# A tuned kernel of two transformer blocks: attention's bias as one line per partition, a later release of scores, a later pool mixing

## The chip, the cores and the metric

The kernel runs on one core of a Trainium2 chip. The metric is the device time of one execution, in microseconds (us). TensorE (PE) multiplies matrices and PEld is its loading of weights. VectorE (DVE) and ScalarE (ACT) do elementwise work, GpSimd (POOL) does some of it and orders small transfers, and SyncE (SP) orders the large transfers from memory. All transfers share the core's sixteen DMA engines.

## The reference, cut to what matters

The reference runs two blocks of layers over 256 tokens of width 1024, batch 1, in fp32. The first block has four layers: pool mixer, attention, convolution, pool mixer. Each begins with an RMS norm that is shifted and scaled by a modulation, a vector computed from a condition (silu(c) times ada_w). The second block has two layers with two feed-forward parts and three kinds of attention each.

Attention of the first block has 16 heads of 64. The tokens are a grid of 4 rows and 64 columns. A query sees, in all four rows, 16 columns around its own, and besides 256 context tokens. A bias is added to the local scores, which depends on the head, the difference of rows and the difference of columns:

```python
s_loc = s_loc + rpb[:, dr_idx, dc_idx]      # na_rpb: 16 heads x 15 x 31
p = softmax(concatenate([s_loc, s_ctx]))
y = ((p_loc @ v_rows + p_ctx @ v_ctx) * silu(g)) @ w_out
```

The pool mixer takes centred means of 2, 4, 8 and 16 tokens in four groups of 256 channels, subtracts the input, multiplies each group with its own 256x256 matrix, scales and gates it, and multiplies with w_out.

## The kernel before, in words

The products are done in three passes with numbers split into a high and a low part. Each weight tile of 512 KB arrives in a buffer `raw`. ScalarE casts it to `whi` (L162) and VectorE computes the rest `wlo` (L163). One product is then three on TensorE: high with high, high with low, low with high.

All weight tiles stand in one list, `units`, in the order in which they are used. Tiles of the modulation's matrix (`ada_w`) are mixed among them; in attention's layer VectorE multiplies and adds these straight from `raw` (`ada_acc`, L556 and L558). `pump_dma` keeps five `raw` buffers ordered on SyncE's queue, `emit_next` writes out the cast of the next unit, and `fill` keeps the casts five weight units ahead of their use. Every engine works through its instructions in the order in which the program writes them.

Attention's layer takes its projections in four chunks of 256 channels: k and v over 512 tokens, then q over 256. Then come four chunks of the gate. Beside these products runs `na_gen`, a generator which does attention itself in small steps. `tick` (L245) is called after each group of 12 products with an estimate of their time. It adds this to a clock, first calls what `later` has put off to a time that is now past, and then lets the generator go on at RATE_N1 = 0.35 steps per us (RATE_N2 = 0.5 from the gates on). `n` counts the 16 steps over pairs of heads and halves of the queries. `s1(n)` writes the scores (TensorE), adds the bias and finds the extreme (VectorE, L1029), and takes the exponential (ScalarE, L1031). `s1b` divides, `s2` turns the weights on TensorE (L1049) and copies them to `na_pt` (L1052), and `s3` multiplies them with v. A step n waits until `ready[0]` is over n // 4, and `ready[0] = j + 1` is set when chunk j's q has been copied to qT (L1120).

`na_bias(p)` prepares the bias of a pair of heads. There are two buffers, so pair p + 2 is prepared when the second step of pair p has been written out. GpSimd orders four transfers (L1005) and then adds the mask of the columns, `namask`, twice (L1007). The result has for each of 128 partitions and each head 6 lines of 64 numbers, of which a step reads 4 lines.

The last pool layer (`in_chunks(8, pool_step, ...)`) has eight chunks, for the groups 3, 2, 1, 0 in turn: first the values u, then the gate. After a u chunk GpSimd makes the means (L802 to L814), and `rest`, put off by POOL_LATE + POOL_MORE * g, subtracts (L823) and splits the result to HH (L341) and HL (L342). `groups((3, 2), msb)` multiplies the first two groups with their matrices and makes the outputs' operands OH and OL (L841 to L848); `out_half` uses them after the last chunk.

Of the kernel before, what the change touches and what calls it, by code (L numbers as in the profile page):

```python
# [13 lines left out]
ALU = mybir.AluOpType  # L14
# [3 lines left out]
P = 128  # L18
# [36 lines left out]
W_OUT = 0.2  # L55
UPD_LATE = 2
RATE_N1 = 0.35
RATE_N2 = 0.5
RATE_A = 0.55
RATE_B = 0.4  # L60
# [54 lines left out]
def kernel(ctx: ExitStack, tc: tile.TileContext, I, csmall, cdec, out):  # L115
    nc = tc.nc
    V, A, G, T = nc.vector, nc.scalar, nc.gpsimd, nc.tensor
# [17 lines left out]
    units = []  # L135
# [94 lines left out]
    def beside(gen, rate):  # L230

        side.append(Side(gen, rate))
        return side[-1]

    def later(us, fn):

        clock["n"] += 1
        pend.append((clock["now"] + us, clock["n"], fn))
        pend.sort(key=lambda x: x[:2])

    def flush():
        while pend:
            pend.pop(0)[2]()
# [106 lines left out]
    namask = cst[:, 640:704]  # L350
# [254 lines left out]
    def pool_units(j, flat):  # L605
        cols = range(0, 2048, 256) if flat else [c + 256 * g for g in (3, 2, 1, 0) for c in (0, 1024)]
        grp = [_Unit("w", I["pool_w_grp"][j, 2 * g:2 * g + 2].rearrange("g (k p) n -> p (g k) n", p=P), 4, 256)
               for g in range(2)]
        wo = I["pool_w_out"][j]
        return w_cols(I["pool_w_in"][j], D, cols), grp, w_cols(wo, D, range(0, D, 256))  # L610

    pin, grp, pout = pool_units(0, True)
    pout = grp + pout
# [17 lines left out]
    cv = w_cols(cw, D, [c + 256 * j for j in range(4) for c in (1024, 2048, 3072, 0)])  # L631
    units += mixed(cv + pair_units(I["conv_w_out"][0]), [])
    pin, grp, pout = pool_units(1, False)
    units += pin[:10] + grp[1:] + pin[10:] + [pout[1], pout[3]] + grp[:1] + [pout[q] for q in (5, 7, 0, 2, 4, 6)]

    def ffn_units(nm, l):
        res = []
# [213 lines left out]
    def norm_half(s, pool):  # L851

        b = msb()
        for q in range(2):
            c0 = 256 * s + q * P
            mm(b[:, q:q + 1], rb[:, c0:c0 + P], ones[:, 0:1], q == 0, True)
        rsqrt(rcol[:, 2 * s:2 * s + 2], b[:, 0:2], 1.0 / D, 2)
        dg = pool.tile([P, 1024 if s else 512], F32, tag="y" if s else "w2", bufs=2 if s else 4, name="w2")[:, 0:256]
        dv = dg.rearrange("p (t q) -> p t q", q=P)
        for q in range(2):  # L860
            V.tensor_scalar(dv[:, q, :], ident, rcol[:, 2 * s + q:2 * s + q + 1], None, op0=ALU.mult)
        halfdg[s] = dg
# [124 lines left out]
    with tc.tile_pool(name="l1", bufs=1) as np_:  # L987
# [4 lines left out]
        rpb = I["na_rpb"]  # L992
        nb = np_.tile([P, 1792], F32, name="nb")
        G.memset(nb[:, 1536:1792], 0.0)
        ready, done = [0], [0]

        def na_bias(p):

            t = nb[:, 768 * (p % 2):768 * (p % 2) + 768]
            tv = t.rearrange("p (e i c) -> p e i c", e=2, c=64)  # L1000
            for e in range(2):
                for half in range(2):
                    off = rpb.offset + ((2 * p + e) * 15 + 5 - half) * 31 + 15 - 63
                    src = bass.AP(rpb.tensor, off, [[1, 64], [31, 6], [1, 64]])
                    G.dma_start(out=tv[64 * half:64 * half + 64, e], in_=src)  # L1005
            for e in range(2):
                G.tensor_tensor(tv[:, e], tv[:, e], namask.unsqueeze(1).to_broadcast([P, 6, 64]), op=ALU.add)  # L1007
            return t

        def na_gen():  # L1010
# [74 lines left out]

        attn = beside(na_gen(), RATE_N1)
        for j in range(4):
            xh, xl = lambda k, tt: HH[:, k, tt * P:(tt + 1) * P], lambda k, tt: HL[:, k, tt * P:(tt + 1) * P]
            if j == 0:
                later(X_COLS, lambda: norm_half(0, np_))  # L1090
                later(X_SPREAD, lambda: spread_half(0))
                make_h(1, 0, qT, X_SPREAD + .3, X_GAP)
                us = get_held(4)
                outs = two_outs(512)
                banks = [mmb(), mmb()]
                for t0 in (256, 0):
                    for q in range(2):
                        fm_unit([o[:, t0:t0 + 256] for o in outs], us[q], 4 * q, KD, lambda k: HH[:, k, t0:t0 + 256],
                                lambda k: HL[:, k, t0:t0 + 256], 256, t0 == 256)
                        if t0 == 0:  # L1100
                            let_go()
                    for q in range(2):
                        tm_unit(banks, us[2 + q], 4 * q, xh, xl, (t0 // P, t0 // P + 1))
                        if t0 == 0:
                            let_go()
                    if t0 == 256:
                        flush()
            else:
                outs = fm_chunk(KD, hx(512), hl(512), 512)
            for m in range(2):  # L1110
                A.copy(kT[:, 2 * j + m, :], outs[m])
            if j:
                banks = tm_chunk(xh, xl, 4)
            for q in range(2):
                A.copy(vv[:, 2 * q:2 * q + 2, 256 * j:256 * j + 256], banks[q].rearrange("p (t f) -> p t f", t=2))
            outs = fm_chunk(KD, hx(256), hl(256), 256)
            for m in range(2):
                o = outs[m]
                back = bass.AP(o.tensor, o.offset + 63, [list(o.ap[0]), [64, 4], [-1, 64]])
                A.activation(qT[:, 2 * j + m, :].rearrange("p (r c) -> p r c", c=64), back, AF.Copy, scale=0.125)  # L1120
            ready[0] = j + 1
        attn.rate = RATE_N2
        gates = []

# [59 lines left out]
    def in_chunks(n, step, between=None):  # L1184

        later(IN_COLS, norm_a)
        later(IN_SPREAD, norm_b)
        first = None
        for q in range(n):
            outs = fm_chunk(KD, hx(258), hl(258), 258)  # L1190
            if q == 0:
                first = outs
                continue
            if q == 1:
                flush()
                step(0, first)
            step(q, outs)
            if between is not None and q in between:
                between[q]()
# [67 lines left out]
    with tc.tile_pool(name="l3", bufs=1) as pp:  # L1267
        sc05 = pool_scale05(pp, 1)
        U = pp.tile([P, KD, 1, 272], F32, name="U")
        SG = pp.tile([P, KD, 256], F32, name="SG")  # L1270
        pp.tile([P, 56], F32, name="pad_o")
        OH, OL = pp.tile([P, KD, 256], F32R, name="OH"), pp.tile([P, KD, 256], F32R, name="OL")
        pool_edges(U)

        def pool_step(q, outs):
            g = 3 - q // 2
            t, col = normed(pp, outs)
            if q % 2 == 0:
                for m in range(2):
                    A.activation(U[:, 2 * g + m, 0, 8:264], t[:, m, :], AF.Identity, bias=col[m])  # L1280
                pool_means(pp, U, g, 1)

                def rest():
                    if rests.pop(g, None):
                        pool_less(U, g)
                        split(YH[:, 2 * g:2 * g + 2, :], YL[:, 2 * g:2 * g + 2, :], U[:, 2 * g:2 * g + 2, 0, 8:264])
                rests[g] = rest
                later(POOL_LATE + POOL_MORE * g, rest)
            else:
                for m in range(2):  # L1290
                    A.activation(t[:, m, :], t[:, m, :], AF.Identity, bias=col[m])
                sg = SG[:, 2 * g:2 * g + 2, :]
                A.activation(sg, t, AF.Tanh, scale=0.5)
                V.scalar_tensor_tensor(sg, sg, 1.0, t, op0=ALU.add, op1=ALU.mult)

        rests = {}

        def groups(order, bank):
            for g in order:
                rests.get(g, int)()  # L1300
            pool_groups(pp, 256, lambda ft: (YH[:, ft, :], YL[:, ft, :]), sc05, SG, OH, OL, order, bank)

        def out_half(c, k0):
            fm_unit(outs[c], get(), k0, KD, lambda k: OH[:, k, :], lambda k: OL[:, k, :], 256, None, 4)

        in_chunks(8, pool_step, {4: lambda: groups((3, 2), msb)})
        outs = [two_outs(256) for _ in range(4)]
        out_half(0, 4)
        out_half(1, 4)
        groups((1, 0), msb)  # L1310
        out_half(2, 4)
        out_half(3, 4)
        for jj in range(4):
            out_half(jj, 0)
            residual(3, jj, outs[jj], 256)
            src = xr[:, 2 * jj:2 * jj + 2, :]
            lay["write"] = HH2, HL2
            operand(jj, gmul)

            def squares(jj=jj, src=src):  # L1320
                acc_sq(nrm, ("acc", "sq"), jj, src, 256)
                acc_sq(fnp, ("acc2", "sq"), jj, src, 256, scale=fg[:, 2 * jj:2 * jj + 2])
            later(ACC_LATE, squares)
# [555 lines left out]
```

## Time and profile before

| | |
|---|---|
| median of 3 runs | 1921.22 us (1914.51 to 1924.17) |
| profiled execution | 1920.95 us, its span 1919.2 us |
| TensorE busy | 1858.4 us, 97% of the span |
| VectorE busy | 1332.1 us, 69% |
| ScalarE busy | 923.9 us, 48% |
| GpSimd busy | 124.8 us, 7% |
| granted clock of TensorE, mean | 0.991 |

The profile is of one execution. The span runs from its first instruction to its last. Windows and starts are in us from the start of the span, and a line such as L1005 is one of the kernel. In a row of the waits the engine at the left stood idle until the one at the right of the arrow was done. A timeline merges like instructions that follow each other, as x2 or x4. The granted clock is 1.00 at 2.4 GHz and 0.50 at 1.2 GHz.

### The profile page before, as it was taken

The page shows a single profiled execution, that of the slowest core. Times are in us where ns is not written, and L with a number is a line of the kernel's source. Part 1 is how long each engine was busy: PE and PEld are TensorE (multiplying, and loading weights), DVE is VectorE, ACT ScalarE, POOL GpSimd, SP SyncE. Part 2 cuts the span into 40 slices and gives each one's busy share as a digit, 9 for nine tenths or more (in the row PEclk, how much of TensorE's full clock was granted, in tenths as well). Part 3 has the DMA queues.
Part 4 walks back from the last instruction along what each step waited for, and adds up shares of the span by engine and source line. Part 5 has one row for each costly group of instructions (what it writes and reads, how often), then busy time and mean ns, then how long its engine had stood idle before and what let it go on. Part 6 is the DMA issues. An engine that isn't in the chain of part 4 may idle for free.

```text
span 1919.2 us, 36616 instructions
## 1 busy us (share of the span) xinstructions
PE 1858.4 (97%) x14939; PEld 1745.9 (91%) x14939; DVE 1332.1 (69%) x2152; ACT 923.9 (48%) x1509; POOL 124.8 (7%) x194
## 2 busy tenths in 40 slices
PE   7999988889999999999999999999999999999998
PEld 4677966679999999999899999999999989999998
DVE  5655776677777887667866777667766786777664
ACT  3333434355555644445754455445444665454442
POOL 3000521100003100010100000000001000000000
PEclk9999999999999999999999999999999999999999
DMA  8684498875555656564645656565656454565663
GB/s 285 222 283 145 99 219 208 211 190 180 162 188 158 182 175 203 169 206 146 167 144 169 209 182 205 192 198 177 205 182 214 146 164 144 176 196 184 204 190 108
DMA packets 319448, 354.38 MB, mean 185 GB/s; under 512 B 12282, under 2 KB 306416, under 8 KB 319280
## 3 DMA queue, kind: packets, MB, share of 16 engines
q1 hardware_dynamic: 315440, 345.48, 56.5%
q0 software_dynamic: 3648, 6.49, 3.9%
q8 instruction: 117, 1.92, 0.4%
q14 instruction: 51, 0.42, 0.1%
q10 hardware_dynamic: 192, 0.07, 0.0%
HBM read 350.95 MB, written 1.05 MB: 183 GB/s over the span
## 4 chain that ended last, share of the span: by engine, by line
PE 80%; DVE 8%; ACT 6%; DMA 4%; issue 2%; POOL 0%; SPq 0%; DVEq 0%; ACTq 0%; POOLq 0%
PE mm L257 72%; DVE wlo L163 3%; PE sc L257 3%; DMA raw<-in_na_w_in_dram 3%; PE ms L257 2%; ACT whi L162 2%; DMA raw<-in_ada_w_dram 1%; PE mm L1049 1%; DVE ada_acc L558 1%; DVE nt L1207 0%; DMA xt<-in_ctx_dram 0%; ACT pw L1585 0%; ACT pw L1666 0%; POOL y L769 0%; ACT w L1031 0%
## 5 line engine op out<-in xcount | busy, mean ns | idle before, releaser
L257 PE MATMUL mm<-HH,whi 128*128 128x256 f32 (+2 forms) x3000 | 872.2, 291 | 1.4 <-ACT U L879 0.8
L257 PE MATMUL mm<-HL,whi 128*128 128x256 f32 (+2 forms) x3000 | 862.8, 288 | 8.1 <-DVE HL L756 3.9
L257 PE MATMUL mm<-HH,wlo 128*128 128x256 f32 (+2 forms) x3000 | 861.6, 287 | 0.0
L163 DVE TENSOR_TENSOR wlo<-raw,whi 128x1024 fp32r<-128x1024 f32 x564 | 666.2, 1215 | 225.5 <-ACT whi L162 224.8
L162 ACT CAST whi<-raw 128x1024 fp32r<-128x1024 f32 x564 | 561.6, 1033 | 202.7 <-PE mm L257 85.2
L257 PEld LDWEIGHTS mm<-HH,whi 128*128 128x128 f32 x3000 | 566.4, 189 | 29.4 <-issue 15.6
L257 PEld LDWEIGHTS mm<-HL,whi 128*128 128x128 f32 x3000 | 567.9, 189 | 19.7 <-DVE HL L771 5.5
L257 PEld LDWEIGHTS mm<-HH,wlo 128*128 128x128 f32 x3000 | 566.0, 189 | 9.2
L257 PE MATMUL mm<-UH,whi 128*128 128x256 f32 x704 | 195.5, 278 | 0.0
L257 PE MATMUL mm<-UL,whi 128*128 128x256 f32 x704 | 195.2, 277 | 0.0
L257 PE MATMUL mm<-UH,wlo 128*128 128x256 f32 x704 | 195.2, 277 | 0.0
L257 PE MATMUL mm<-whi,HH 128*128 128x256 f32 x640 | 184.9, 289 | 0.0
L257 PE MATMUL mm<-wlo,HH 128*128 128x256 f32 x640 | 179.0, 280 | 1.1 <-DVE wlo L163 1.1
L257 PE MATMUL mm<-whi,HL 128*128 128x256 f32 x640 | 178.9, 279 | 0.0
L257 PEld LDWEIGHTS mm<-UL,whi 128*128 128x128 f32 x704 | 132.9, 189 | 0.0
L257 PEld LDWEIGHTS mm<-UH,whi 128*128 128x128 f32 x704 | 132.1, 188 | 0.0
L257 PEld LDWEIGHTS mm<-UH,wlo 128*128 128x128 f32 x704 | 132.1, 188 | 0.0
L257 PEld LDWEIGHTS mm<-whi,HH 128*128 128x128 f32 x640 | 120.8, 189 | 5.4 <-issue 5.2
L257 PEld LDWEIGHTS mm<-wlo,HH 128*128 128x128 f32 x640 | 120.8, 189 | 1.5 <-DVE wlo L163 1.3
L257 PEld LDWEIGHTS mm<-whi,HL 128*128 128x128 f32 x640 | 120.7, 189 | 0.0
L558 DVE SCALAR_TENSOR_TENSOR ada_acc<-raw,csil,ada_acc 128x1024 f32<-128x1024 f32 x49 | 63.7, 1299 | 15.0 <-DMA raw<-in_ada_w_dram 14.2
L341 ACT CAST UH<-t 128x512 fp32r<-128x512 f32 x44 | 27.3, 621 | 96.4 <-DVE t L1375 96.4
(324 smaller groups left out, 1793.8 us busy)
## 6 DMA issues: line engine op xcount, KB each, us to landing
raw<-in_w_in_dram SPq DMA_DIRECT2D x120, 512.0 KB, 4.5
raw<-in_ada_w_dram SPq DMA_DIRECT2D x96, 512.0 KB, 5.6
raw<-in_ffn_w_gate_dram SPq DMA_DIRECT2D x88, 512.0 KB, 4.8
raw<-in_ffn_w_up_dram SPq DMA_DIRECT2D x88, 512.0 KB, 4.9
raw<-in_ffn_w_down_dram SPq DMA_DIRECT2D x80, 512.0 KB, 4.5
raw<-in_pool_w_in_dram SPq DMA_DIRECT2D x32, 512.0 KB, 5.1
raw<-in_na_w_in_dram SPq DMA_DIRECT2D x32, 512.0 KB, 4.8
raw<-in_conv_w_in_dram SPq DMA_DIRECT2D x32, 512.0 KB, 4.9
```

The costliest lines, as they stand in the source:

```text
L162: A.copy(u.hi, u.raw)
L163: V.tensor_tensor(u.lo, u.raw, u.hi.bitcast(F32), op=ALU.subtract)
L257: T.matmul(o, lhsT=lhsT, rhs=rhs, start=start, stop=stop, skip_group_check=True)
L341: A.copy(hi, src)
L558: V.scalar_tensor_tensor(hold["a"], raw[:, 0, :], cc, hold["a"], op0=ALU.mult, op1=ALU.add)
L1049: T.transpose(b[:, k * P:(k + 1) * P], L[:, k * P:(k + 1) * P], flip)
```

## The change

The bias is loaded differently. For each of the 16 transfers that are left (two per pair) a partition receives, for both heads, one run of 219 numbers, placed at 165 to 383 of that head's 384. The six lines of 64 lie in this run 31 numbers apart. GpSimd then adds the mask while it moves each line to its place, from position 165 + 31 i to 64 i, for both heads in one instruction. The line i = 4 overlaps with its own place and is done in two halves. So there are seven additions per pair.

The release of a chunk's scores, `ready[0] = j + 1`, is put off with `later` by Q_LATE = 2.5.

In the last pool layer `groups((3, 2), msb)` is called after the sixth chunk and not after the fifth, and the weights' order in `units` follows this.

```diff
--- before.py
+++ after.py
@@ -55,6 +55,7 @@
 W_OUT = 0.2
 UPD_LATE = 2
 RATE_N1 = 0.35
+Q_LATE = 2.5
 RATE_N2 = 0.5
 RATE_A = 0.55
 RATE_B = 0.4
@@ -631,7 +632,7 @@
     cv = w_cols(cw, D, [c + 256 * j for j in range(4) for c in (1024, 2048, 3072, 0)])
     units += mixed(cv + pair_units(I["conv_w_out"][0]), [])
     pin, grp, pout = pool_units(1, False)
-    units += pin[:10] + grp[1:] + pin[10:] + [pout[1], pout[3]] + grp[:1] + [pout[q] for q in (5, 7, 0, 2, 4, 6)]
+    units += pin[:12] + grp[1:] + pin[12:] + [pout[1], pout[3]] + grp[:1] + [pout[q] for q in (5, 7, 0, 2, 4, 6)]
 
     def ffn_units(nm, l):
         res = []
@@ -997,14 +998,17 @@
         def na_bias(p):
 
             t = nb[:, 768 * (p % 2):768 * (p % 2) + 768]
-            tv = t.rearrange("p (e i c) -> p e i c", e=2, c=64)
-            for e in range(2):
-                for half in range(2):
-                    off = rpb.offset + ((2 * p + e) * 15 + 5 - half) * 31 + 15 - 63
-                    src = bass.AP(rpb.tensor, off, [[1, 64], [31, 6], [1, 64]])
-                    G.dma_start(out=tv[64 * half:64 * half + 64, e], in_=src)
-            for e in range(2):
-                G.tensor_tensor(tv[:, e], tv[:, e], namask.unsqueeze(1).to_broadcast([P, 6, 64]), op=ALU.add)
+            line = t.rearrange("p (e c) -> p e c", e=2)
+            for half in range(2):
+                off = rpb.offset + (2 * p * 15 + 5 - half) * 31 + 15 - 63
+                src = bass.AP(rpb.tensor, off, [[1, 64], [15 * 31, 2], [1, 219]])
+                G.dma_start(out=line[64 * half:64 * half + 64, :, 165:384], in_=src)
+
+            for i in range(6):
+                for c, n in ((0, 32), (32, 32)) if i == 4 else ((0, 64),):
+                    o, f = 64 * i + c, 165 + 31 * i + c
+                    m = namask[:, c:c + n].unsqueeze(1).to_broadcast([P, 2, n])
+                    G.tensor_tensor(line[:, :, o:o + n], line[:, :, f:f + n], m, op=ALU.add)
             return t
 
         def na_gen():
@@ -1118,7 +1122,7 @@
                 o = outs[m]
                 back = bass.AP(o.tensor, o.offset + 63, [list(o.ap[0]), [64, 4], [-1, 64]])
                 A.activation(qT[:, 2 * j + m, :].rearrange("p (r c) -> p r c", c=64), back, AF.Copy, scale=0.125)
-            ready[0] = j + 1
+            later(Q_LATE, lambda j=j: ready.__setitem__(0, j + 1))
         attn.rate = RATE_N2
         gates = []
 
@@ -1303,7 +1307,7 @@
         def out_half(c, k0):
             fm_unit(outs[c], get(), k0, KD, lambda k: OH[:, k, :], lambda k: OL[:, k, :], 256, None, 4)
 
-        in_chunks(8, pool_step, {4: lambda: groups((3, 2), msb)})
+        in_chunks(8, pool_step, {5: lambda: groups((3, 2), msb)})
         outs = [two_outs(256) for _ in range(4)]
         out_half(0, 4)
         out_half(1, 4)
```

## Rows read from the trace of the kernel before

**Rows 1.** Page: busy time; granted clock and DMA share in 40 slices
```profile
PE 1858.4 (97%) x14939; PEld 1745.9 (91%) x14939; DVE 1332.1 (69%) x2152; ACT 923.9 (48%) x1509; POOL 124.8 (7%) x194
...
PEclk9999999999999999999999999999999999999999
DMA  8684498875555656564645656565656454565663
```

**Rows 2.** Busy us by stretch (PE, PEld, DVE, ACT, POOL), clock, DMA share
```profile
299.00:349.40 50.40, 45.15 (x285) 34.41 (x285) 33.56 (x56) 19.91 (x40) 9.27 (x12) 0.94 0.82 208
...
400.00:440.00 40.00, 34.55 (x259) 26.54 (x257) 29.46 (x59) 21.02 (x42) 0.00 (x0) 1.00 0.57 181
220.00:400.00 180.00, 163.32 (x1084) 131.84 (x1082) 120.09 (x197) 73.00 (x140) 47.10 (x55) 0.94 0.84 203
```

**Rows 3.** Waits of TensorE, 220 to 440 us: total, times, longest
```profile
PE sc L257 <- ACT qT L1120: 10.8, 2, 5.5
PE ms L257 <- ACT na_pt L1052: 4.0, 3, 2.6
PE sc L257 <- DVE na_m L1029: 3.8, 1, 3.8
PE mm L1049 <- DVE w L1042: 2.0, 1, 2.0
```

**Rows 4.** Chain of waits, 280 to 300 us: start, us, what
```profile
283.99 13.47 DMA raw<-in_na_w_in_dram
...
298.53 0.29 ACT qT L1120
```

**Rows 5.** Busy time by stretch, granted clock third from the end
```profile
260.20:266.90 6.70, 4.66 (x19) 3.46 (x17) 4.88 (x11) 3.61 (x9) 1.75 (x3) 0.50 0.76 236
...
618.60:621.90 3.30, 3.30 (x18) 3.30 (x17) 1.72 (x4) 1.85 (x3) 1.15 (x2) 0.50 0.43 137
```

**Rows 6.** DMA by queue and issue, 220 to 400 us
```profile
q1 hardware_dynamic: 17705, 33.12, 54.0%
q0 software_dynamic: 1536, 3.15, 29.8%
...
nb<-in_na_rpb_dram POOLq DMA_DIRECT2D x32, 96.0 KB, 7.2
```

**Rows 7.** The same view, 856 to 863 us, second block's bias
```profile
q0 software_dynamic: 307, 0.82, 41.8%
...
bb<-in_b_rel_bias_dram POOLq DMA_DIRECT2D x4, 48.0 KB, 3.7
```

**Rows 8.** GpSimd by line, whole span: busy us, mean ns | idle before
```profile
L1007 POOL TENSOR_TENSOR nb<-nb,cst 128x384 f32<-128x384 f32 x16 | 20.0, 1249 | 72.4 <-DMA nb<-in_na_rpb_dram 68.4 <-issue 4.1
...
L814 POOL TENSOR_TENSOR sa<-sa,cst 128x8 f32<-128x8 f32 x8 | 4.3, 563 | 0.2
```

**Rows 9.** GpSimd in order of time: start us, us, what
```profile
235.74 1.98 POOL L1007 TENSOR_TENSOR nb<-nb,cst 128x384 f32<-128x384 f32 x1 [0.77 <-DMA nb<-in_na_rpb_dram]
...
265.15 2.58 POOL L1005 DMA_DIRECT2D nb<-in_na_rpb_dram  x4 [11.41 <-DVE na_m L1029]
...
278.74 1.07 POOL L1007 TENSOR_TENSOR nb<-nb,cst 128x384 f32<-128x384 f32 x1 [3.91 <-DMA nb<-in_na_rpb_dram]
```

**Rows 10.** VectorE in order of time, 590 to 640 us
```profile
599.55 4.12 DVE L163 TENSOR_TENSOR wlo<-raw,whi 128x1024 fp32r<-128x1024 f32 x2
...
605.92 1.27 DVE L163 TENSOR_TENSOR wlo<-raw,whi 128x1024 fp32r<-128x1024 f32 x1 [1.59 <-ACT whi L162]
...
617.14 0.69 DVE L342 TENSOR_TENSOR HL<-U,HH 128x512 fp32r<-128x512 f32 x1 [0.68 <-ACT HH L341]
...
624.34 1.29 DVE L848 TENSOR_TENSOR OL<-y,OH 128x512 fp32r<-128x512 f32 x2
```

**Rows 11.** TensorE in order of time, 611 to 618 us
```profile
611.68 0.28 PE L257 MATMUL ms<-HH,whi 128*128 128x256 f32 x1
...
617.16 0.38 PE L257 MATMUL ms<-HH,whi 128*128 128x256 f32 x1 [3.92 <-ACT HH L341]
```

## The prediction

> **What bounds the kernel now.** I read the page first: TensorE is busy 97% of the span, and its granted clock is full nearly throughout, but the DMA line is high in the sixth to ninth slice [rows 1]. Those are attention in the first block, about 220 to 440 us, so I asked for busy time by stretch there. From 220 to 400 us TensorE is busy 163.32 of 180 us at a mean clock of 0.94, and the DMA engines are at a share of 0.84 for only 203 GB/s [rows 2]. The waits of TensorE name the places: 10.8 us on qT, 3.8 us on the maxima na_m, 2.0 us on the weights w, and 4.0 us on na_pt at the end of the stage [rows 3]. ScalarE makes qT, but the chain shows that it isn't the cause: at 283.99 a weight tile is ordered, it lands 13.47 us later, its cast goes first on ScalarE, and qT follows it [rows 4]. The chains of the waits at 255 and 344 us have the same form. The DMA view says why a 512 KB tile takes so long. The bias of attention, 3.15 MB, holds 29.8% of the sixteen engines over 180 us, which is 53.6 us, while 33.12 MB of weights hold 54.0%, or 97.2 us [rows 6]. So the bias moves 59 GB/s while it runs and the weights 341. Behind each of the three long waits the granted clock is 0.50 for some 6.7 us (the first at 260.2 [rows 5], two more from 297.8 and 348.9).
>
> The second place is the last pool layer. There TensorE begins the products of group 2 at 617.16 after 3.92 us of waiting for the cast HH [rows 11], and a stretch of 3.30 us at clock 0.50 follows [rows 5].
>
> **The change part by part.**
>
> *Bias by DMA.* Now each pair of heads takes four DMAs of 64 partitions by 6 runs of 256 B: 8 pairs make 12,288 runs. After it there are two DMAs of 64 by 2 runs of 219 numbers, 876 B: 2,048 runs and 1.79 MB. The nearest row is the second block's bias, which has runs of 768 and 1,024 B from sources that overlap in the same way (beside one table of longer runs): 0.82 MB held 41.8% of 7 us, 2.93 us, or 280 GB/s [rows 7]. At that rate the new lines cost 6.4 us. At the present cost for one run (53.6 us / 12,288) they cost 8.9 us, and at the present cost for one byte 30.5 us. I take 7, because the second block's runs are almost the same [rows 7]; the far end is no more than 30.5. The DMA engines then need 97 + 7 = 104 us for what TensorE does in some 155, and the landing of 13.47 us should go towards the 5 us that weights take elsewhere. Eight us earlier is more than any of the waits (5.5 us the longest), so the waits of 10.8 + 3.8 + 2.0 = 16.6 us lose their cause. With them go three stretches at half clock, 3 x 6.7 / 2 = 10.0 us. At 30.5 us the landing would shrink by 23.1/53.6 of its excess, 3.6 us, leaving nearly 2 us of each of the two waits on qT: the gain is then about 18 us and not 26.6.
>
> *Bias on GpSimd.* Two adds of 384 columns per pair become seven: five of 128 columns, two of 64. One now takes 1249 ns in the mean, and an 8-column operation takes up to 563 ns [rows 8]. A straight line between the two gives 0.8 us for 128 and 0.7 for 64 columns, 5.4 us per pair where 2.5 stood. The bounds are 7 x 0.56 = 3.9 us and 7 x 1.98 = 13.9 us, the latter if every one takes what the slowest takes now [rows 9]. Two DMA issues fewer give back 1.3 us (2.58 for four). Hidden or not: the third pair's bias is issued at 265.15 and finished at 279.8 [rows 9], and its first reader follows the scores released near 298.9, so about 19 us of cover are left. What is queued behind these adds on GpSimd is the next pair's bias alone. At the upper bound, with a landing of 7.2 us [rows 6], it would take 1.3 + 7.2 + 13.9 = 22.4 us of the 33.7: still hidden, and after the stage is shorter, just so. Cost 0.
>
> *Scores released later.* The code's clock advances only at the ticks of the products. After chunks 0 to 2 the next tick is a half unit of 512 columns, 2.616 us, and the release was acted on only there; a delay of 2.5 expires at that same tick. For these three chunks the order stays what it was. Only after chunk 3 are the ticks 1.308 us, so that its four score steps move back by one or two ticks. Counting the steps through the gate chunks gives three steps left to be forced at the end, not two. The extra one exposes a transpose-copy-product chain that had one tick of cover: I take 1.5 us, between 0 (ScalarE is there anyway) and 2.6 (two ticks, also the longest such wait now, [rows 3]). Of the 4.0 us now waited on na_pt, the first wait had a late weight tile before it; about 1 us should go and the rest stay. Sum for the tail: 0.5 us worse.
>
> *Pool groups one chunk later.* A chunk of 48 products now stands between. The products of one group are 12, and from 611.68 they run at steps of 0.12 us [rows 11], so a chunk is about 5.7 us. TensorE would reach group 2 at 613.1 + 5.7 = 618.8, and HL is written by 617.83 [rows 10]; that operation comes before the groups in VectorE's queue both times. The whole 3.92 us goes, about 0.3 us on HL behind it, and 3.30 / 2 = 1.65 us of clock: 5.9 us. The margin is 1 us. What is late next would be the groups' outputs: the last OL now ends at 625.63 [rows 10], with the output's products after two more chunks; one chunk, 5.7 us, is left, and that is about the distance from group 2's end near 620 to OL. So at worst a fraction of 1 us comes back. The bounds are 0 and 5.9; I take 5.5.
>
> **The sum.** 16.6 + 10.0 + 5.5 - 0.5 = 31.6 us if nothing takes the place. Something will: VectorE, at 120.09 busy us [rows 2], would be filled to 78% in 153 us, and small waits of its queue's order are to be expected. I leave 4 us for them, about what the tail, at 74% of VectorE [rows 2], waits now. That makes 27.6 us. The profiled execution took 1920.95 us (span 1919.2), which is the median of the timed runs (1921.22) within 0.3: forecast 1893 us.
>
> **Rivals.**
>
> *VectorE takes half of it.* Its share in the busiest stretch is 74% (29.46 of 40) [rows 2]. If it can't go higher, 120 us want 162 and the stage ends 18 us sooner rather than 27; with a few us more of GpSimd's disturbance the total is some 12 to 18 us: 1903 to 1909. For it: its queue runs in program order and the sums of the modulation (ada_acc) stand among the casts. Against it: most of its idle time there is behind late weights, by the chain.
>
> *The lines are no cheaper.* If 2,048 runs hold the DMA engines as long as 12,288 did, only the pool part and the tail are left: 5 us, 1916. Against it: the second block's lines, at 280 GB/s [rows 7].
>
> *Slower: GpSimd holds up VectorE.* Two splits of weights (wlo) took 4.12 us while GpSimd was adding, and one alone took 1.27 [rows 10]: 1.6 times as long. So each us of GpSimd's adds may cost VectorE 0.38 us. At 1.98 us an add, 56 adds are 111 us instead of 20, VectorE has 155 busy us, and at 74% the stage takes 209 us: 29 more, less 5.5 for the pool, 1944. It turns to a loss when the adds exceed about 68 us in sum, 1.2 us each; the straight line above says 0.77. VectorE's own attention steps read PSUM and were not stretched, which speaks against it too. The Trainium skill (GPSIMD Engine Reference, section Specifications) says that the two engines share their SBUF interface and contend when VectorE has two SBUF inputs; wlo has two, and the pair at 599.55 agrees.
>
> **How the numbers follow.** Forecast 0.70, with its own range of 1886 to 1902; VectorE's half 0.16; lines no cheaper 0.06; slower 0.05; the rest, 0.03, a larger gain. The range of 1884 to 1908 takes in the forecast, the gain of 18 us, and most of the second case. Telling apart 0.5% means 9.6 us: under 1911.6 is faster. Nearly all of the first two cases, and the last, lie there: 0.87; same 0.08; slower 0.05.
>
> **What would show it.** In the changed profile: q0's share over the stage at 3 to 6%; na_w_in landing near 5 us; no wait on qT over 2 us and no half clock between 250 and 360 us; GpSimd's adds at 0.5 to 0.8 us; the third pair's bias done within 15 us of its issue; no wait at the pool groups and full clock there; attention's last wait on na_pt somewhat longer. The forecast is wrong if waits on w or na_m grow to more than 8 us in sum, or if the two-input splits are stretched for most of the stage.

## The result, and the profile after

The changed kernel takes 1899.41 us (median of 4 runs, 1891.86 to 1900.62), the kernel before 1922.70 in the same comparison; the ratio is 0.9875, 95% interval 0.9851 to 0.9899. That is 23.3 us less, inside the range; 27.6 were forecast. The parts came out otherwise: attention gained more than was forecast, the pool part cost time.

From the page after, the lines that answer to [rows 1] (busy time; DMA share by slice). TensorE is busy 3.8 us less in a span that is 20.6 us shorter, and slices 6 to 9 of the DMA line are lower.

```profile
PE 1854.6 (98%) x14939; PEld 1744.0 (92%) x14939; DVE 1330.8 (70%) x2152; ACT 923.9 (49%) x1509; POOL 139.0 (7%) x218
...
DMA  8684287754564656564545655566666545566563
```

Busy time by stretch, to set beside [rows 2] (PE, PEld, DVE, ACT, POOL, then clock, DMA share, GB/s):

```profile
299.00:349.40 50.40, 50.40 (x338) 39.37 (x336) 36.39 (x63) 24.23 (x48) 18.09 (x26) 1.00 0.74 234
400.00:440.00 40.00, 36.31 (x287) 33.13 (x286) 28.48 (x50) 22.31 (x39) 0.19 (x4) 0.96 0.54 168
220.00:400.00 180.00, 178.97 (x1266) 145.69 (x1267) 139.69 (x240) 85.76 (x165) 63.18 (x80) 1.00 0.72 227
```

From 220 to 400 us TensorE is now busy 178.97 us of 180 at full clock, where it was busy 163.32 at 0.94. The stretch from 299 to 349.4 us has no idle time of TensorE left, with more products in it. VectorE rises to 139.69 of 180 us, 78%, the share that the forecast had worked out; the clock of 0.96 from 400 to 440 belongs to the wait in the tail. The waits of TensorE from 220 to 440 us, first one row from before that belongs to [rows 3] and stood in the tail too, then all rows after:

```profile
PE mm L1049 <- DVE na_m L1041: 1.5, 2, 1.3
```

```profile
PE mm L1053 <- DVE na_m L1045: 3.6, 1, 3.6
PE mm L1053 <- ACT na_pt L1056: 0.8, 1, 0.8
PE ms L258 <- ACT na_pt L1056: 0.2, 1, 0.2
```

The waits on qT, na_m after the scores, and w are gone. One of 3.6 us is left, at 404.7 to 408.3, in the tail. It is for the reciprocal of na_m (L1045, L1041 before), which stands in VectorE's queue behind a sum of the modulation and a split of weights (405.00 to 407.41). The DMA view of 220 to 400 us beside [rows 6]:

```profile
q1 hardware_dynamic: 21792, 38.80, 65.8%
q0 software_dynamic: 768, 1.80, 5.9%
...
raw<-in_na_w_in_dram SPq DMA_DIRECT2D x24, 512.0 KB, 5.0
...
nb<-in_na_rpb_dram POOLq DMA_DIRECT2D x16, 109.5 KB, 3.4
```

The bias holds 5.9% of 180 us, 10.6 us and not 53.6; the sixteen engines carry 38.80 MB of weights in the stretch and not 33.12, and a tile of na_w_in lands in 5.0 us in the median. Before, its row was this:

```profile
raw<-in_na_w_in_dram SPq DMA_DIRECT2D x22, 512.0 KB, 6.4
```

The 13.47 us of [rows 4] were thus among the longest landings, not a usual one. Of all weight tiles ordered in the stretch the slowest landed in 13.4 us before and in 7.1 after. GpSimd's adds, one row of all ([rows 8]: 16 of 1249 ns) and the third pair in order of time ([rows 9]):

```profile
L1011 POOL TENSOR_TENSOR nb<-nb,cst 128x128 f32<-128x128 f32 (+1 forms) x56 | 44.7, 810 | 30.9 <-DMA nb<-in_na_rpb_dram 28.4
```

```profile
259.91 1.19 POOL L1005 DMA_DIRECT2D nb<-in_na_rpb_dram  x2 [6.75 <-DVE na_m L1033]
264.55 5.26 POOL L1011 TENSOR_TENSOR nb<-nb,cst 128x128 f32<-128x128 f32 x7 [3.44 <-DMA nb<-in_na_rpb_dram]
```

The third pair's bias is done at 269.8, 9.9 us after its issue; before, that was 14.7. One pair was late: at 308.8 us VectorE waited 2.2 us for the fifth pair's adds, and TensorE waited for nothing there.

To see where the time went I cut the span at products of TensorE that both kernels have: the product that spreads the norm before attention, the end of attention's last product, the norm's first product behind the convolution (after the first chunk of the last pool layer), and the norm's first product behind that layer (as far into the next one). Before, and then after (start us, us, what):

```profile
221.48 0.67 PE L257 MATMUL ms<-w,ones 128*128 128x256 f32 x2
...
436.33 3.67 PE L257 MATMUL ms<-na_pt,vv 128*64 128x256 f32 x30 [0.28 <-ACT na_pt L1052]
...
590.59 0.50 PE L257 MATMUL ms<-ones,accs 128*128 128x1 f32 x4
...
677.19 1.05 PE L257 MATMUL ms<-ones,accs 128*128 128x1 f32 x8 [1.72 <-DVE accs L427]
```

```profile
223.46 0.62 PE L258 MATMUL ms<-w,ones 128*128 128x256 f32 x2
...
412.05 4.41 PE L258 MATMUL ms<-na_pt,vv 128*64 128x256 f32 x32
...
567.04 0.50 PE L258 MATMUL ms<-ones,accs 128*128 128x1 f32 x4
...
655.47 1.05 PE L258 MATMUL ms<-ones,accs 128*128 128x1 f32 x8 [1.71 <-DVE accs L428]
```

| part | before | after | difference |
|---|---|---|---|
| start to the spread product | 221.5 | 223.5 | +2.0 |
| attention, to the end of its last product | 218.5 | 193.0 | -25.5 |
| convolution | 150.6 | 150.6 | 0.0 |
| last pool layer | 86.6 | 88.4 | +1.8 |
| rest of the span | 1242.0 | 1243.1 | +1.1 |

The code of the first and the last row is the same in both kernels. In all the profiles below the first row lies between 221.5 and 229.5 us and the last between 1235.0 and 1243.6, so single times of whole kernels can't tell 3 us apart; the parts can. Attention with the scores released at once and the new bias lies within 190.9 to 191.4 us in five profiles. The pool layer takes 86.4 to 87.2 us in five profiles with the groups after the fifth chunk, and 88.0 to 89.0 in eight with the groups after the sixth (no_means aside).

### The profile page after: what moved, and what is told of

Same layout as the page of the kernel before. It is cut to its first block, busy times and chain, and to the rows that moved or that the text cites. A ratio compares the mean times of both kernels' runs of the same rounds, so it can differ in the third digit from the quotient of the medians.

```text
span 1898.6 us, 36611 instructions
## 1 busy us (share of the span) xinstructions
PE 1854.6 (98%) x14939; PEld 1744.0 (92%) x14939; DVE 1330.8 (70%) x2152; ACT 923.9 (49%) x1509; POOL 139.0 (7%) x218
## 4 chain that ended last, share of the span: by engine, by line
PE 80%; DVE 8%; ACT 6%; DMA 2%; issue 2%; POOL 1%; SPq 0%; DVEq 0%; ACTq 0%; POOLq 0%
PE mm L258 73%; DVE wlo L164 3%; PE sc L258 3%; PE ms L258 2%; ACT whi L163 2%; DMA raw<-in_ada_w_dram 1%; PE mm L1053 1%; DVE nt L1211 1%; ACT w L1035 0%; DMA xt<-in_ctx_dram 0%; ACT pw L1589 0%; ACT pw L1670 0%; DMA raw<-in_na_w_in_dram 0%; POOL y L770 0%; ACT HH L342 0%
## 5 line engine op out<-in xcount | busy, mean ns | idle before, releaser
L1377 ACT ACTIVATE th<-t 128x512 f32<-128x512 f32 x44 | 27.8, 632 | 88.5 <-DVE t L1375 88.5
```

The source lines that it names most:

```text
L1377: A.activation(th, t1, AF.Tanh, scale=0.5)
```

## The experiments

In the first expectations theory 1 is that the gain is the bias's share of the DMA engines alone; the later release costs a little, and the pool's wait only moves. The rival is that release and pool give their share too. The table has the cuts as above, from each kernel's profile, and the ratio to the kernel before. Where a kernel's median is near another's, only the parts are compared.

| kernel | median us | ratio (95%) | attention | pool layer |
|---|---|---|---|---|
| bias_only | 1896.28 | 0.9846 (0.9823 to 0.9869) | 190.9 | 87.2 |
| pool_only | 1925.20 | 1.0003 (0.9991 to 1.0014) | 219.5 | 88.0 |
| release_now | 1897.55 | 0.9863 (0.9848 to 0.9877) | 191.4 | 88.1 |
| no_loads | 1903.74 | 0.9896 (0.9880 to 0.9913) | 198.9 | 86.6 |
| rest_later | 1900.49 | 0.9888 (0.9858 to 0.9918) | 193.0 | 88.8 |
| no_means | 1895.50 | 0.9857 (0.9833 to 0.9882) | 195.6 | 83.7 |
| adds_double | 1900.94 | 0.9885 (0.9859 to 0.9910) | 196.1 | 88.9 |
| rest_later_now | 1897.50 | 0.9868 (0.9838 to 0.9898) | 191.2 | 88.5 |
| short_runs | 1899.20 | 0.9866 (0.9851 to 0.9881) | 194.0 | 89.0 |
| edges_once | 1897.57 | 0.9846 (0.9822 to 0.9869) | 191.3 | 86.4 |
| edges_once_5 | 1898.01 | 0.9858 (0.9842 to 0.9874) | 190.9 | 88.4 |
| rows_apart | 1896.12 | one run | 193.8 | 86.6 |

**One part alone.** bias_only is the kernel before with the new na_bias; pool_only is the kernel before with the two lines of the pool part.

> The kernel before with the new bias alone: lines of 219 numbers, seven adds; scores released at once, pool groups after the fifth chunk. Theory 1 (the gain is the bias's share of the DMA engines, and nothing else gains): 24 to 26 us less than before, attention's part from the spread product to the norm behind the convolution about 343.6 us long (369.1 before, 343.6 in the changed kernel), the last pool layer as before at 86.6 us from its first norm product to the next norm product. Rival (the later release carries part of it, and the pool part too): less than 18 us.

> The kernel before with the pool groups one chunk later and nothing else. Theory 1 (the wait of 3.9 us goes and comes back as waits for casts and for the operands OH and OL): within 3 us of before, the last pool layer 87 to 89 us long instead of 86.6, with a wait on a cast (whi) before its end. Rival (the prediction's step was right and the changed kernel lost elsewhere): 5 us less, the layer 81 us long.

Both came out as theory 1 says, bias_only with somewhat more gain than the 24 to 26 us expected (28.0 by the medians). The bias alone takes 27.7 us off attention (218.5 to 190.9), more than the whole change does. The pool part alone makes the layer 1.4 us longer and leaves the kernel where it was. The expectations speak of attention with the convolution: 341.4 us in bias_only.

**The release undone.**

```diff
-            later(Q_LATE, lambda j=j: ready.__setitem__(0, j + 1))
+            ready[0] = j + 1
```

> The changed kernel with a chunk's scores released at once and not 2.5 us later. Theory 1 (by the count of ticks only the last chunk's scores move): scores of the first three chunks start after the same products, no new wait on qT above 1 us, and the tail loses its wait of 3.6 us on na_m or exchanges it for waits of 3 to 4 us in sum on na_pt, as before; total within 3 us of the changed kernel, rather below it. Rival (the later release is what took away the waits on qT): waits on qT come back, 3 to 5 us at two or three places, 6 to 15 us more.

No wait on qT came back. The waits of TensorE from 220 to 440 us:

```profile
PE ms L258 <- ACT na_pt L1056: 2.2, 1, 2.2
PE mm L1053 <- ACT na_pt L1056: 1.0, 1, 1.0
```

3.2 us on na_pt stand where 3.6 us on na_m and 1.0 on na_pt were; attention is 1.6 us shorter. Over the profiles whose attention is otherwise alike it is 190.9 to 191.4 us without the delay (five) and 193.0, 193.0 and 195.6 with it (the changed kernel, rest_later, no_means): the delay costs about 2 us or more, and gives nothing once the weights are in time.

**The transfers left out.** The kernel before without the transfers of pairs 2 to 7, with all adds:

```diff
-            for e in range(2):
+            for e in range(2 if p < 2 else 0):
                 for half in range(2):
...
```

> The kernel before, which leaves out the bias's transfers for pairs 2 to 7 (the first two pairs' remain, and all adds of the mask). Theory 1: the waits on qT at the second and third chunk go, landing of na_w_in falls to about 5 us, attention's part shrinks to 343 to 349 us, so 20 to 26 us less than before. Rival (the adds on GpSimd or the order of the scores made the difference): attention's part stays above 360 us.

Old adds, old release, and attention is 19.6 us shorter. With the convolution it is 349.6 us, just beyond the 343 to 349 expected. Its DMA rows and its waits:

```profile
q0 software_dynamic: 384, 0.79, 6.6%
...
raw<-in_na_w_in_dram SPq DMA_DIRECT2D x23, 512.0 KB, 4.9
```

```profile
PE sc L257 <- DVE na_m L1029: 3.5, 1, 3.5
PE mm L1049 <- DVE w L1042: 2.5, 1, 2.5
PE ms L257 <- ACT na_pt L1052: 2.2, 1, 2.2
```

The waits on qT are gone. The first wait, 3.5 us on na_m with 2.5 on w behind it, has stayed, as the two first pairs' transfers have; the longest landing of a weight tile is still 13.1 us. In bias_only, where these are lines too, that wait is gone. So each wait goes with the transfers that run before it.

**What made the old transfers dear.** short_runs fetches each new line as three transfers of 73 numbers. rows_apart is the kernel before with `[[1, 64], [65, 6], [1, 64]]` as the source pattern in place of `[[1, 64], [31, 6], [1, 64]]` (and the start held inside the table).

> The changed kernel with each line of 219 numbers fetched as three runs of 73 (292 B) in separate transfers: the same 1.79 MB, 6,144 runs and not 2,048, six transfers per pair and not two. If the DMA engines' time goes by the run (53.6 us for 12,288 runs before): 27 us, near 15% of the stage, landing of na_w_in 6 to 7 us, attention's part 195 to 202 us. If it goes by the byte: 10 to 12 us as with whole lines (10.6 us), attention's part within 2 us of 193.0.

> The kernel before, whose bias transfers read their six runs 65 numbers apart and not 31, so that the runs of one partition no longer overlap in memory; the bias that it adds is not the reference's. Same 12,288 runs of 256 B, same 3.15 MB, same four transfers per pair. If the overlap within a partition's runs made the old form dear (short_runs showed that runs of 292 B cost no more than lines): the bias falls from 53.6 us of the DMA engines to 15 to 25 us, and attention's part from 218.5 to 193 to 205 us. If the form itself does (packets of 8 and 16 runs of 256 B, six per partition): 45 to 55 us as before, attention's part 214 to 220 us.

The bias's queue and its landing in short_runs, then in rows_apart:

```profile
q0 software_dynamic: 1536, 1.80, 6.6%
...
nb<-in_na_rpb_dram POOLq DMA_DIRECT2D x48, 36.5 KB, 4.3
```

```profile
q0 software_dynamic: 1536, 3.15, 15.0%
...
nb<-in_na_rpb_dram POOLq DMA_DIRECT2D x32, 96.0 KB, 4.9
```

Runs of 292 B, three times as many, cost 11.9 us, hardly more than lines (10.6): not the count of runs. And the old form, with its 12,288 runs of 256 B 65 numbers apart, costs 15.0% of 180 us, 27.0 and not 53.6, a little over the 15 to 25 expected; attention falls to 193.8 us. Half the price of the old form was thus, by this one profile, how its six runs lay: 31 numbers apart, each overlapping the next. Whether the overlap as such or the small distance counts, the runs don't tell. With a bias of 27.0 us attention gains 24.7 us, and 27.7 with one of 10.6 and the same release (bias_only). The 2.9 us between them hold waits on qT, 1.8 us in sum, which bias_only doesn't have: most of the gain comes with the first half of the price, and not all.

**GpSimd's adds.** After each line's add the same once more on its result:

```diff
                     G.tensor_tensor(line[:, :, o:o + n], line[:, :, f:f + n], m, op=ALU.add)
+                G.tensor_tensor(line[:, :, o:o + n], line[:, :, o:o + n], m, op=ALU.add)
```

> The changed kernel with each of the seven additions of the mask followed by the same addition once more in place: 112 instead of 56, about 90 us of GpSimd instead of 44.7. Theory 1 (these additions are hidden): attention's part from the spread product to its last product stays within 3 us of 193.0. Rival, the slower case of the prediction (each us of additions costs VectorE 0.38 us, and a loss begins near 68 us of additions): 45 us more cost 17 us of VectorE and attention's part grows by 8 to 20 us, with waits on VectorE (w, na_m, na_pt).

```profile
L1011 POOL TENSOR_TENSOR nb<-nb,cst 128x128 f32<-128x128 f32 (+1 forms) x56 | 40.5, 724 | 30.7 <-DMA nb<-in_na_rpb_dram 30.1
L1012 POOL TENSOR_TENSOR nb<-nb,cst 128x128 f32<-128x128 f32 (+1 forms) x48 | 38.2, 795 | 3.8
```

The new line stands outside the inner loop, so that the line done in two halves gets one more add and not two: there are 104 adds and not the 112 expected. They take 78.7 us and not 44.7, and attention is 3.1 us longer, just over theory 1's bound of 3. In no_means, whose attention is the changed kernel's, it is 2.6 us longer too; in both the half clock behind the wait in the tail lasts 6.8 us and not 3.4, which is 1.7 us of it. A wait of 1.3 us on w is new (0.5 in no_means), so that up to 1.4 us can be the adds'. The slower rival of the prediction falls: 34 us more of adds at its price of 0.38 would be 13 us more of VectorE, and VectorE is busy 140.64 us from 220 to 400 us where it was 139.69.

**The pool layer.** In the changed kernel TensorE's waits in it are these:

```profile
PE sc L258 <- ACT whi L163: 1.4, 1, 1.4
PE mm L258 <- ACT OH L843: 0.8, 1, 0.8
PE mm L258 <- DVE OL L849: 0.8, 1, 0.8
PE sc L258 <- DVE wlo L164: 0.8, 1, 0.8
```

With three more, of 0.7, 0.5 and 0.3 us, they come to some 5.2 us in seven places. Before there were two, of 3.9 and 0.3 us. A stretch at half clock is there both times: 618.6 to 621.9 before ([rows 5]), 609.3 to 612.5 after, behind the waits on whi and wlo. So neither the wait nor the clock was gained. The chain of waits from 594 to 608 us (start, us, what) shows the first:

```profile
597.14 1.10 POOL sa L803
...
600.34 1.76 POOL sb L815 x4
...
602.12 0.44 DVE U L824
...
602.63 0.63 ACT HH L342
...
604.35 0.92 ACT nt L1295 x2
...
605.29 0.63 ACT SG L1297
605.92 0.94 ACT whi L163
```

The second weight tile of the last chunk (the eighth; the expectations count from 0 and call it chunk 7) is cast at 605.92, behind SG, nt and the split HH of group 1 in ScalarE's queue. HH waits for the subtraction U on VectorE and this for GpSimd's means, which end at 602.1; VectorE itself is busy with two splits of weights until 601.3, 3.31 us for both. Before, the same order stood in ScalarE's queue (HH of group 1 at 628.96, the next cast of a weight tile at 632.16), and TensorE waited for none of it. That the 3.92 us it had waited for group 2 were the cover is argued from this.

In the expectations that follow theory 1 is this order of ScalarE's queue; theory 2 is GpSimd's work, which stretches VectorE's operations and holds the subtraction back. rest_later writes the split of groups 3 to 1 out later (POOL_MORE 1.6 to 3.0). no_means leaves out GpSimd's levels and edge corrections in this layer. edges_once, made from the kernel before with the new bias, does four edge corrections in one, and edges_once_5 is the same with the groups after the sixth chunk. The lines of no_means and edges_once in one cut (the names at the right are not in the code, and the last line stands in both):

```diff
-        for lev in range(g):
+        for lev in range(g if ns == 2 else 0):                      # no_means
-        for m in range(2):
+        if ns == 1:                                                 # edges_once
+            ends = bass.AP(cur.tensor, cur.offset + 8, [list(cur.ap[0]), [272, 2], [248, 2], [1, 8]])
+            eg = edge[:, g:g + 1, :].rearrange("p o (e c) -> p o e c", e=2).to_broadcast([P, 2, 2, 8])
+            E.tensor_tensor(ends, ends, eg, op=ALU.mult)
+        for m in range(2 if ns == 2 else 0):
             for e0, c0 in ((0, 8), (8, 256)):
```

> The changed kernel with POOL_MORE = 3.0 for 1.6, so that the subtraction and split of groups 3, 2 and 1 are written out later (group 1: 6.0 instead of 4.6 us on the code's clock after its chunk), behind the casts of the weights. Theory 1 (the waits of 1.4 and 0.8 us in chunk 7 came from casts queued behind that split, which itself waits for the means on GpSimd): these two waits shrink below 0.5 us each, the half clock behind them goes, and the layer falls from 88.4 us to 84 to 86. Rival (VectorE and ScalarE have too much work in this layer, so that a wait removed at one place comes back at the next): 87.5 to 89 us, with new waits of 2 us or more elsewhere.

> The changed kernel, which leaves out in the last pool layer the means beyond the first addition of neighbours and the correction at the edges: GpSimd is nearly silent there. Theory 2 (GpSimd's additions stretch VectorE's two-input operations, two splits took 4.1 us instead of 2.5, and hold the subtraction back): splits of weights take 1.2 to 1.3 us each throughout, the waits in chunk 7 and at the groups go, the layer falls to 81 to 83 us, the 5.5 us that were forecast. Theory 1 alone (order of ScalarE's queue): at least 1.5 us of waits remain in chunk 7 and the layer stays above 85 us.

In rest_later the two waits in the last chunk vanish and the layer is no shorter, 88.8 us. TensorE now waits elsewhere:

```profile
PE ms L258 <- ACT ncol L1210: 1.5, 1, 1.5
PE mm L258 <- ACT HH L1166: 1.3, 1, 1.3
PE mm L258 <- DVE wlo L164: 1.1, 2, 0.6
PE ms L258 <- DVE wlo L164: 0.5, 1, 0.5
```

Theory 1's order of the queue explains where a wait stands, not its sum: its rival holds. In no_means the waits in the last chunk vanish too, no stretch at half clock is left, and the layer falls by 4.7 us to 83.7; theory 2 had said 81 to 83. The splits of weights from 565 to 610 us, in the changed kernel and then in no_means:

```profile
L164 DVE TENSOR_TENSOR wlo<-raw,whi 128x1024 fp32r<-128x1024 f32 x11 | 16.9, 1552 | 4.0 <-ACT whi L163 3.9
```

```profile
L164 DVE TENSOR_TENSOR wlo<-raw,whi 128x1024 fp32r<-128x1024 f32 x15 | 18.0, 1228 | 4.5 <-ACT whi L163 4.4
```

1552 ns against 1228 in the mean. So 4.7 us of this layer hang on GpSimd's work there. That this work kept the later groups from their forecast 5.5 us is not shown, since no run leaves the means out with the groups after the fifth chunk. How much of the 4.7 us is the stretching of VectorE and how much the later means, this run doesn't separate, since it removes both; 1.0 and 0.8 us of waits on OH and OL remain in it. The Trainium skill (GPSIMD Engine Reference, section Specifications) has the two engines contend when VectorE reads two inputs from SBUF. The two means agree with it here; in attention it hardly shows, with 1249 ns for a split in the changed kernel and 1292 with the adds of adds_double (216 to 400 us).

> The kernel before with the new bias, and in the last pool layer the correction of the means at both edges of both tiles in one operation on GpSimd and not in four (pool groups after the fifth chunk, scores released at once). Theory 2 (GpSimd's length of work holds this layer back): GpSimd is done 1.2 us sooner per group, the wait of 3.9 us at the groups falls to 2 to 3 us, the layer from 87.2 to 84 to 86 us. Rival (the wait hangs on VectorE's queue alone): 86 to 87.5 us, the wait unchanged.

> The same with the pool groups after the sixth chunk. Theory 2: the splits that GpSimd stretches are fewer, the waits in chunk 7 (1.4 and 0.8 us) fall below 1 us in sum and those at the second pair of groups go; the layer takes 84 to 86 us where it took 88.0 to 88.4, and the later groups are no longer worse than the earlier. Rival (the order of the queues alone): 87.5 to 88.5 us. Total 1891 to 1896 us by theory 2.

With the groups after the fifth chunk, the wait of 3.91 us stays as it is, as the rival said; the layer is 86.4 us. After the sixth, 1.13 and 0.75 us remain in the last chunk and the layer is 88.4. The test is weaker than it was meant to be: one correction takes 1.12 us where four took 1.55, so that GpSimd is done with the groups 3 and 2 only 0.4 us sooner and not 1.2. But the trace of the kernel before agrees with the rival on the wait for group 2: its means end at 612.2, and VectorE subtracts them at 615.71, behind SG and a split of weights.

> The changed kernel with POOL_MORE = 3.0 and the scores released at once, the sum of two single edits. Theory 1: attention's part 191 us (193.0 with the delay), the last pool layer 84 to 86 us (88.4), so 4 to 6 us less than the changed kernel, about 1894 us. Rival (waits only move): within 2 us of the changed kernel.

Only the release counts in it: attention 191.2 us, the layer 88.5. Theory 1 said 4 to 6 us less, and it is 2, as its rival had it.

The experiments point to the new bias alone, with release and pool as they were. bias_only's median, 1896.28, is the lowest of the timed kernels that leave nothing out, but its interval overlaps the changed kernel's; that it is better by some 3 us rests on the parts (2.1 us in attention, 1.2 in the pool layer), not on the whole.

## Why the prediction was right, and where it was not

That the total came within 4.3 us of the forecast is in part luck, for two errors offset each other: attention gained 25.5 us and not 22.1, and the pool part lost 1.8 where 5.5 were to be gained.

*Bias by DMA: right.* Its 26.6 us without anything in their place are close to what the bias alone gave, 27.7. The lines cost 10.6 us and not 7, above the value by the run, 8.9, and far below the bound of 30.5. That mattered little: 16.4 us more, in rows_apart, took 2.9 us from the gain. The rule by the run that gave 8.9 was itself wrong, since the way the runs lay had doubled the old price. The forecast's claim that at 30.5 us a gain of only 18 would be left was too dark: at 27.0 us rows_apart gained 24.7.

*Bias on GpSimd: right in its cost of 0.* An add took 810 ns where 0.77 us was worked out. That is close, but the straight line began at 563 ns, read as the most that an 8-column add takes; it is the mean of eight, and single ones took 198 to 1182 ns. The third pair took 9.9 us where 12 to 14 could be added up, well inside its cover. The fifth had none left, and only VectorE waited, 2.2 us. The slower rival's remark that VectorE's attention steps were not stretched holds for those that read PSUM (L1029, 682 to 692 ns), not for the scaling L1042: 1.03 us at 279.07, while GpSimd added, and 0.49 at 278.47.

*Scores released later: right in size, not in place.* The order of the first three chunks stayed (the scores of step 12 start some 120 products after those of step 11, some 96 in release_now; up to step 11 the two kernels agree within 4), and the delay cost about 2 us where 1.5 were forecast. The wait is on na_m, not on na_pt as foreseen, and it brings a half clock of its own. In order, the half clock in the changed kernel's tail, in adds_double's tail, and in the changed kernel's pool layer:

```profile
407.90:411.20 3.30, 2.91 (x14) 2.94 (x15) 2.60 (x6) 0.59 (x1) 0.00 (x0) 0.50 0.89 295
...
408.90:415.80 6.90, 5.75 (x25) 4.90 (x27) 3.40 (x11) 1.80 (x4) 0.00 (x0) 0.51 0.72 230
...
609.30:612.50 3.20, 3.20 (x17) 3.20 (x17) 2.97 (x5) 2.83 (x7) 0.00 (x0) 0.50 0.49 159
```

*The 4 us for VectorE: too much.* VectorE reached 78% of the stretch, and the waits of TensorE from 220 to 400 us come to 1.0 us. The wait of 3.6 us in the tail is for VectorE's queue too, but it goes with the delay (release_now), and so I count it there. The forecast for attention was 16.6 + 10.0 - 0.5 - 4 = 22.1; it was 25.5. The trace accounts for that: TensorE's waits from 220 to 440 us fell by 17.5 us, from 22.1 in sum to 4.6, and one stretch at half clock of 3.4 us stands where three of 6.7 stood, 8.4 us of clock.

*Pool groups one chunk later: wrong, the step that failed.* "The whole 3.92 us goes" was right for that wait, and group 2's products follow group 3's without a pause. "What is late next would be the groups' outputs" was the failure: late next were the casts of the last chunk's weights, which stand behind the split of group 1 in ScalarE's queue, and then the outputs OH and OL of the second two groups, 1 and 0; those of the first two came in time. The forecast followed the products' own operands and not the other work of the two engines that make them. 5.5 us were forecast as gain, between 0 and 5.9, and 1.8 us were lost (1.4 in pool_only): some 5.2 us of waits in place of 4.2, and a half clock as long as before. With both parts as measured, the sum is -25.5 + 1.8 = -23.7 us; the medians say -23.3.

The rival of half a gain by VectorE falls with the waits, the dear lines with 5.9%, the slower case with adds_double.

## What to carry to other kernels

When transfers crowd each other, price them by the time that they hold the DMA engines and not by their bytes: a small table held them more than half as long as weights of ten times its bytes, and waits that bore the name of a ScalarE copy were its doing. A wait at one product in a chain of engines that all work in program order is cover for everything else in these queues; before counting it as gain, look up what the next weight cast stands behind. Parts cut at the same instruction in several profiles tell 1 to 2 us where whole times can't.

## What was not expected of the hardware

12,288 runs of 256 B, the six of a partition 124 B apart in memory, held the DMA engines 53.6 us, and as many 260 B apart 27.0 us. Lines of 876 B took 10.6 us, and the same bytes in runs of 292 B 11.9 us. A wait of the same 3.6 us was followed by a half clock of 3.4 us in the changed kernel and of 6.8 us in adds_double, so one profile alone is uncertain by 1.7 us per such wait. GpSimd's means went with splits of weights of 1552 ns on VectorE in the pool layer (1228 without them), while 34 us more of its adds in attention left VectorE's busy time within 1 us.
